# Queries and keys stored once per pair of heads, loaded in halves into even and odd partitions, with the transfer queue in program order from the first head's loads

## The chip, the cores and the metric

The kernel runs on one core of a Trainium2 chip. The time is that of one execution in device microseconds (us); shorter is better. A core has five engines with instruction streams of their own, which wait for each other by semaphores: TensorE (PE, matrix products; PEld is its loading of stationary operands), VectorE (DVE), ScalarE (ACT), GpSimd (POOL) and SyncE (SP), which here only issues transfers (DMAs). ACT issues transfers too; SPq and ACTq in the profile are these issues.

## The reference

One encoder block on a sequence of 1024 positions with 1024 channels, in float32:

```python
h = rmsnorm(x, g_mix) * (1 + scale1) + shift1          # scale, shift, gate from silu(c) @ w_ada
qa, ka, va, qb, kb, vb, ga, gb = split(h @ w_in)       # 8 + 8 heads of 64; two gates of 1024
oa = mixture_of_dilations(qa, ka, va, rel_bias)        # 8 heads: windows 128, 512, 2048 at strides 1, 4, 16
ob = neighbourhood_attention_2d(qb, kb, vb, na_rpb)    # 8 heads: 8 x 16 windows on a 16 x 64 grid
x = x + gate1 * ((sigmoid(ga) * (oa @ w_branch_dil) + sigmoid(gb) * (ob @ w_branch_na)) @ w_out)
h2 = rmsnorm(x, g_ffn) * (1 + scale2) + shift2
u = depthwise_conv3(h2 @ w_up)
x = x + gate2 * ((gelu(u_g) * u_v) @ w_down)
y = rmsnorm(x, g_final)
```

The outputs of an attention head are sums over exp(q·k/8 + bias) within its windows.

## The kernel before

**Numbers in two halves.** Float32 values go through PE as a high half (the value rounded to the matmul's format, made by ACT with a copy, L57 or L366) and a low half (the difference, made by DVE or POOL, L368, L61). A product is three matmuls: high by high, high by low, low by high; for the gates these are L84, L85 and L86.

**The stages, in order.** 0 to about 150 us: norm, conditioning, the values' projections and the first query/key projections (among them L308 and L310), with the order of all engines written out by hand. To about 297 us: the remaining query/key projections for pairs of heads, as products with seven instead of eight block multiplications (the generator `products`, L505 to L507; its sums and copies are L511 to L530); here a scheduler of the compiler orders each engine's instructions from its own estimates, and loads of weights (L723) go through SP. Then `fill(11)`, the first steps of the gate projections, and from 301 us the attention: 102 slots in a loop, each with transposes (T), scores (S) and outputs (O) of several heads in turn, with gate steps in between (`fill`). The rest (branch, output, up and down projections) runs to the end.

**Queries and keys.** A product gives two heads' queries (y = 0) or keys (y = 1) at once, head A on partitions 0 to 63 and head B on 64 to 127. `qk_evict` (pairs 0 to 3, the dilated heads) and `na_evict` (pairs 4 to 7, the neighbourhood heads) split them into halves (`split_qk`) and store them from ACT's queue into `q_scr`, `[16 heads, 3, 2, 64, 1024]`: for each head a tile of queries (high over low), one of the keys' high half twice, and one of their low half twice. So `qk_evict` issues two transfers for queries (L382) and four for keys (L379), one for each head and, for keys, each half; `na_evict` two times two (L406, L403). In all 80 stores: 64 of 256 KB and 16 of 512 KB.

`qk_load` brings a head back with three transfers of 512 KB on SP (L411) into the tiles `qs`, `ks` and `kl`: 128 partitions, the upper 64 the second copy. A score (dilated heads: L1028 and L1029) is then two matmuls over 128 partitions, (high; low) queries by (high; high) keys, and the same by (low; low) keys.

**Before the first score.** SP's and POOL's order is written by hand in one block: the first head's loads, `lnm`, the biases of head 0 (L701, L702), its values `vv` (L689 to L692; ACT copies them in two halves at L789, and splits follow), the biases of head 1. The next part of the program opens manual order for PE, ACT and DVE (`att`) and for SP (`att_sp`), ahead of `fill(11)`. Among the instructions of `fill(11)` are SP's load of weight tile 26 (L65) and the store of a gate tile `gs` (L1326, copied out by ACT at L1324); the load of tile 27 follows. These and the first head's block are separate hand-written pieces, and between pieces the scheduler may choose. In the compiled program tile 26, `gs` and tile 27 stand in SP's stream ahead of the first head's loads. A weight tile is split on ACT at L961 when its turn comes.

**Completion semaphores.** In the compiled program SP's and ACT's transfers share eight completion semaphores in turn, and a transfer first waits for the landing of the one eight before it in the scheduled order.

Of the kernel before, what the change touches and what calls it, by code (L numbers as in the profile page):

```python
# [10 lines left out]
FT = mybir.dt.float32  # L11
# [6 lines left out]
S = 1024  # L18
# [11 lines left out]
def hybrid_encoder(tc, xT, c, w_ada, small, w_in, p1_bias, p23_bias, na_bias, ln2_mult, ident, w_br, w_out,  # L30
                   w_up, w_down, out):
    nc = tc.nc
    act, dve, pool, pe, sp = nc.scalar, nc.vector, nc.gpsimd, nc.tensor, nc.sync
# [3 lines left out]
    dram = tc.alloc_tile_pool(name="scr", bufs=1, space=DRAM)  # L37

    def f(ap):
        return ap.bitcast(FT)  # L40
# [47 lines left out]
    halves = [slice(0, 512), slice(512, 1024)]  # L88
# [54 lines left out]
    def pair_load(j, i):  # L143
        wt = wada_tile(j)
        sp.dma_start(wt, w_ada[j][:, 2 * i:2 * i + 2])
        return [wt[:, t] for t in range(2)]
# [65 lines left out]
    def x_load(hf):  # L212
        x = []
        for k in range(0, KT, 2):
            if hf == 0:
                x2k = qkpool.tile([128, 2, 512], FT, name=("ks", "qb")[k // 6], bufs=(4, 2)[k // 6])
                raw_h[0].append(x2k)
                sp.dma_start(x2k, xT[hf, k // 2])
                x += [x2k[:, i] for i in range(2)]
            else:  # L220
                for i in range(2):
                    x.append(h_tile(FT))
                    sp.dma_start(x[-1], xT[hf, k // 2][:, i])
        return x
# [76 lines left out]
    def v_wide(*sts):  # L301
        ps = [ps_s.tile([128, 512], FT, name="pv", bufs=3) if len(sts) == 1 else ps_g.tile([128, 512], FT, name="pj")
              for _ in sts]
        for k in range(KT):
            whi, wlo = (t[:, :, k] for t in v_all)
            for st, p in zip(sts, ps):
                hhi, hlo = (t[:, st % 4 * 128:st % 4 * 128 + 128] for t in h[st // 4, k])
                pe.matmul(p, hhi, whi, start=k == 0, stop=False)  # L308
                pe.matmul(p, hhi, wlo, start=False, stop=False)
                pe.matmul(p, hlo, whi, start=False, stop=k == KT - 1)  # L310
        return ps
# [47 lines left out]
        banks = [ps_s.tile([128, 512], FT, name="pv", bufs=3) for _ in range(2)]  # L359
        return [banks[st // 2][:, st % 2 * 256:st % 2 * 256 + 256] for st in range(4)]  # L360

    q_scr = dram.tile([16, 3, 2, 64, S], FT, name="qks")

    def split_qk(y, dst, src):
        hi, lo = dst
        act.activation(hi, src, AF.Copy, scale=(1.0, 0.125)[y])  # L366
        if y:
            dve.scalar_tensor_tensor(lo, src, 0.125, f(hi), OP.mult, OP.subtract)  # L368
        else:
            dve.tensor_tensor(lo, src, f(hi), OP.subtract)  # L370

    def qk_evict(pr, y, hf, p, tag):
        st = qkpool.tile([128, 2, 512], FR, name=tag)
        split_qk(y, (st[:, 0], st[:, 1]), p)
        for i in range(2):
            a, dst = slice(64 * i, 64 * i + 64), q_scr[2 * pr + i][..., halves[hf]]
            if y:
                for x_ in range(2):
                    act.dma_start(dst[1 + x_].rearrange("b p s -> p b s"),  # L379
                                  f(st)[a, x_:x_ + 1].to_broadcast([64, 2, 512]))  # L380
            else:
                act.dma_start(dst[0].rearrange("b p s -> p b s"), f(st)[a])  # L382

    na_st = {}

    def na_evict(pr, y, hf, p):
        first = (pr, y) not in na_st
        if first:
            na_st[pr, y] = [qkpool.tile([128, S], FR, name="qs") for _ in range(2)]
        st = na_st[pr, y]  # L390
        if y:
            split_qk(y, [t.rearrange("p (w t r) -> p r w t", w=16, t=16)[:, 2 * hf:2 * hf + 2] for t in st],
                     p.rearrange("p (r w t) -> p r w t", r=2, w=16))
        else:
            for r in range(2):
                split_qk(y, [t.rearrange("p (c w r t) -> p r c w t", c=4, w=16, r=4)[:, 2 * hf + r] for t in st],
                         p.rearrange("p (r w c t) -> p r c w t", r=2, w=16, c=4)[:, r])
        if not first:
            for x_, t in enumerate(na_st.pop((pr, y))):
                for i in range(2):  # L400
                    src, dst = f(t)[64 * i:64 * i + 64], q_scr[2 * pr + i]
                    if y:
                        act.dma_start(dst[1 + x_].rearrange("b p s -> p b s"),  # L403
                                      src.rearrange("p (o s) -> p o s", o=1).to_broadcast([64, 2, S]))
                    else:
                        act.dma_start(dst[0, x_], src)  # L406

    def qk_load(head):
        qk = [qk2.tile([128, S], FR, name=n) for n in ("qs", "ks", "kl")]
        for y in range(3):  # L410
            sp.dma_start(f(qk[y]), q_scr[head, y].rearrange("b p s -> (b p) s"))  # L411
        return qk

    def q_blocks(qk):
        q = qk2.tile([128, S], FR, name="qb")
        for r in range(4):
            pool.tensor_scalar(q.rearrange("p (b r j) -> p r b j", b=8, r=4)[:, r],
                               f(qk[0][:, 256 * r:256 * r + 256]).rearrange("p (b j) -> p b j", b=8), 1.0, None,
                               OP.mult)
        qk.append(q)  # L420
# [113 lines left out]
    with tc.manual_schedule(engines={e.engine for e in (sp, act, dve, pool, pe)}):  # L534
        x = [x_load(0)]
# [103 lines left out]
        rows = {n: pair_load(*pairs[n]) for n in range(7)}  # L639
# [10 lines left out]
        for y in range(2):  # L650
            qk_evict(0, y, 0, qk_psum[y], "kl")
# [42 lines left out]
        def v_raw(load, head):  # L694
            vv = sm_pool.tile([128, 16, 128], FR, name="vv", bufs=2)
            load(head, f(vv[:, :, 64:128]))
            return vv

        def dil_bias(head):
            bt = sm_pool.tile([128, 896], FT, name="bias", bufs=4)  # L700
            sp.dma_start(bt[:, 0:512], p1_bias[head])  # L701
            sp.dma_start(bt[:, 512:896], p23_bias[head])  # L702
            return bt
# [33 lines left out]
        for n, step in enumerate(v_steps[:10]):  # L737
            if step is None:
                for ks in (slice(0, 4), slice(4, 8)):
                    for hv in range(2):  # L740
                        v_split(v_raws[hv], (dve, pool), ks, v_w[hv])
                raw[0] = p_load(0)
                ps = [ps_g.tile([128, 512], FT, name="pj") for _ in range(2)]
                for k in range(KT):
                    for p, w in zip(ps, qk_w):
                        product(p, w, lambda k: h[1, k], ks=[k])
                for y in range(2):
                    qk_evict(0, y, 1, ps[y], "kl")
                va_chunks(slice(0, 512))
                t_sums()  # L750
                prep = [a_operands(raw.pop(0), 4, p_home, p_sts[0], spot=p_spot)]
            else:
                p = v_wide(*step[1:])
            row_pairs(done_rows, row_ends[n])
            if step is not None:
                for st, pp in zip(step[1:], p):
                    v_out(step[0], st, pp, queue=act)
            done_rows = row_ends[n]
            if n in PREP:
                next(prep[0])  # L760
# [94 lines left out]
    qk2 = tc.alloc_tile_pool(name="qk2", bufs=2, reuse_waits="tile")  # L855
    at_pool = tc.alloc_tile_pool(name="at", bufs=2, reuse_waits="tile")
    sm_pool = tc.alloc_tile_pool(name="sm", bufs=2, reuse_waits="tile")
    with tc.manual_schedule(engines={sp.engine, pool.engine}):
        qks = {0: qk_load(0)}
        lnm = sm_pool.tile([128, 384], FT, name="lnm", bufs=1)  # L860
        sp.dma_start(lnm, ln2_mult)
        biases = {0: dil_bias(0)}
        values = {0: v_raw(va_load, 0)}
        biases[1] = dil_bias(1)
        pool.tensor_tensor(biases[0][:, 512:896], biases[0][:, 512:896], lnm, OP.add)
        q_blocks(qks[0])
# [38 lines left out]
    def settle():  # L905
# [6 lines left out]
        scored.clear()  # L912

    qks[1] = qk_load(1)
    side, second, count, credit = collections.deque(), collections.deque(), [0, 0], [0]

# [447 lines left out]
    def fill(n, asides=True):  # L1364
        for _ in range(n):
            next(steps, None)
            if asides:
                catch_up(550)
# [2 lines left out]
        for job, args in jobs:  # L1371
            job(*args)

    att = contextlib.ExitStack()
    att.enter_context(tc.manual_schedule(engines={e.engine for e in (pe, act, dve)}))
    att_sp = contextlib.ExitStack()
    att_sp.enter_context(tc.manual_schedule(engines={sp.engine}))
    fill(11)
    for s in range(LAST + 1):
        now[0] = s  # L1380
# [18 lines left out]
    o = [[opool.tile([128, 4, S], FR, name=f"o0{n}") for n in ("hi", "lo")]]  # L1399
# [76 lines left out]
    rows, sums = {}, {}  # L1476
# [33 lines left out]
    for i in range(2 * KT):  # L1510
        m, hf = divmod(i, 2)
# [16 lines left out]
        p = []  # L1528
# [441 lines left out]
    with tc.manual_schedule(engines={dve.engine}):  # L1970
        for hf, cs in ((0, slice(0, 512)), (1, slice(0, 256)), (1, slice(256, 512))):
            n = cs.stop - cs.start
            late = []
            for m in range(KT):
                if hf == 0 and m + 2 < KT:
                    end_w[m + 2] = end_weights(m + 2)
                p = ps.tile([128, 512], FT, name="pj", bufs=6)[:, :n]
# [25 lines left out]
        hf, cs, bc = before  # L2003
# [8 lines left out]
        dst = out[:, :, halves[hf]][:, :, cs]  # L2012
# [114 lines left out]
```

## Time and profile before

| | |
|---|---|
| runs before | 1497.62, 1498.62 (median), 1502.53 us |
| profiled execution | 1500.84 us |
| its span, first to last instruction | 1499.0 us |
| mean granted PE clock | 0.99 |
| busy: PE, DVE, POOL, ACT | 1453.7, 949.3, 859.0, 792.4 us |
| transfers | 249.52 MB, 166 GB/s in the mean |

The profile's rows come from one execution. "L505 PE MATMUL pj<-op,kl" is the instruction of line 505 on PE, with output and inputs by the program's names. A bracket such as [7.57 <-DMA ks<-qks] says how long the engine had stood idle just before, and what ended it. The granted clock is the share of full speed at which PE was allowed to run.

### The profile page before, as it was taken

Reading aid. Unit: us, or ns where it says so; the run is one execution under the profiler, and the core shown is the slowest. Engines: PE = TensorE matmul, PEld = TensorE weight load, DVE = VectorE, ACT = ScalarE, POOL = GpSimd, SP = SyncE. Lnnn points to the kernel's source line nnn. Section 1 sums busy time; section 2 is a strip of 40 time slices with the busy share of each in tenths; the row PEclk is TensorE's granted clock in tenths of the full one; section 3 lists DMA queues with packets and bytes.
Section 4 is the critical chain, followed back from the end, with each engine's and each line's share of the span. In section 5 each row is a group of like instructions: output and inputs, shape, how many; then the busy total and the mean of one; then the engine's idle time right before and its main releaser. Section 6 shows DMA issues by size and latency. Waiting matters only on the chain.

```text
span 1499.0 us, 21282 instructions
## 1 busy us (share of the span) xinstructions
PE 1453.7 (97%) x7308; PEld 1225.6 (82%) x7308; DVE 949.3 (63%) x1793; ACT 792.4 (53%) x1479; POOL 859.0 (57%) x706
## 2 busy tenths in 40 slices
PE   9999999979999989999999999999999999999998
PEld 8888777768888878888888878888888888887788
DVE  7687433335655666766625798666666667787865
ACT  6625533257777766763335555444444447575542
POOL 4155655443545466522258858766666676988712
PEclk9999999989999999999999999999999999999999
DMA  9589467774655789667734413222222234532213
GB/s 370 211 317 329 136 180 235 206 243 129 204 160 158 230 250 283 199 224 261 232 134 155 134 43 108 93 84 76 85 76 85 84 134 144 197 123 89 100 45 113
DMA packets 133588, 249.52 MB, mean 166 GB/s; under 512 B 47813, under 2 KB 60741, under 8 KB 133445
## 3 DMA queue, kind: packets, MB, share of 16 engines
q1 hardware_dynamic: 120408, 218.99, 44.1%
q10 hardware_dynamic: 13072, 29.17, 6.7%
q8 instruction: 58, 0.95, 0.3%
q14 instruction: 50, 0.40, 0.1%
HBM read 185.60 MB, written 68.29 MB: 169 GB/s over the span
## 4 chain that ended last, share of the span: by engine, by line
PE 66%; DMA 12%; DVE 10%; ACT 4%; issue 3%; POOL 3%; ACTq 2%; SPq 1%; DVEq 0%; POOLq 0%
PE pj L505 12%; PE pj L506 11%; PE pj L507 11%; PE pj L84 7%; PE pj L86 7%; PE pj L85 7%; DMA qks<-qs 3%; PE O L1299 1%; DMA oraw<-w_ada 1%; PE T L1044 1%; DMA gs<-gs 1%; PE O L1109 1%; PE O L1056 1%; DMA qks<-kl 1%; PE T L1092 1%
## 5 line engine op out<-in xcount | busy, mean ns | idle before, releaser
L61 POOL TENSOR_TENSOR wlo<-wraw,whi 128x512 fp32r<-128x512 f32 (+1 forms) x90 | 114.8, 1299 | 132.3 <-ACT whi L57 130.4
L505 PE MATMUL pj<-op,wsh 128*128 128x512 f32 x408 | 158.5, 390 | 1.9 <-ACT wsh L57 1.9
L506 PE MATMUL pj<-op,wsh 128*128 128x512 f32 x408 | 158.7, 389 | 0.5 <-DVE op L1546 0.5
L507 PE MATMUL pj<-op,wsl 128*128 128x512 f32 x408 | 157.4, 389 | 0.0
L61 POOL TENSOR_TENSOR wsl<-big,wsh 128x512 fp32r<-128x512 f32 (+1 forms) x86 | 111.9, 1326 | 44.7 <-ACT wsh L57 39.8
L84 PE MATMUL pj<-h,whi 128*128 128x512 f32 x272 | 116.4, 428 | 0.0
L86 PE MATMUL pj<-h,wlo 128*128 128x512 f32 x272 | 107.6, 396 | 0.0
L85 PE MATMUL pj<-h,whi 128*128 128x512 f32 x272 | 107.5, 395 | 0.0
L1756 DVE SCALAR_TENSOR_TENSOR big<-pj,sm,big 128x512 f32<-128x512 f32 (+2 forms) x183 | 94.8, 562 | 16.5 <-ACT big L1750 15.6
L887 DVE CUSTOM_DVE_ANT_0 P<-S,bias 128x256 f32<-128x256 f32 x128 | 49.2, 421 | 78.1 <-PE S L1029 39.8
L505 PEld LDWEIGHTS pj<-op,wsh 128*128 128x128 f32 x408 | 76.6, 188 | 18.6 <-ACT wsh L57 2.7
L505 PE MATMUL pj<-op,whi 128*128 128x512 f32 x232 | 90.7, 391 | 0.3 <-ACT wc L511 0.3
L506 PE MATMUL pj<-op,whi 128*128 128x512 f32 x232 | 90.4, 390 | 0.2 <-DVE op L1576 0.2
L507 PE MATMUL pj<-op,wlo 128*128 128x512 f32 x232 | 90.3, 389 | 0.0
L506 PEld LDWEIGHTS pj<-op,wsh 128*128 128x128 f32 x408 | 76.6, 188 | 16.7 <-DVE op L1546 0.9
L61 POOL TENSOR_TENSOR wsl<-wraw,wsh 128x384 fp32r<-128x384 f32 (+1 forms) x46 | 56.8, 1256 | 57.5 <-ACT wsh L57 53.2
L507 PEld LDWEIGHTS pj<-op,wsl 128*128 128x128 f32 x408 | 76.6, 188 | 16.0 <-POOL wsl L61 0.2
L888 ACT ACTIVATE P<-P,st 128x256 f32<-128x256 f32 x128 | 64.0, 502 | 38.1 <-DVE st L887 37.8
L901 DVE TENSOR_TENSOR tl<-T,th 128x512 fp32r<-128x512 f32 (+3 forms) x120 | 76.0, 648 | 5.2 <-ACT th L897 5.2
L57 ACT ACTIVATE whi<-wraw 128x1024 fp32r<-128x1024 f32 (+2 forms) x48 | 47.5, 993 | 55.0 <-PE pj L85 33.7
L1750 ACT ACTIVATE big<-pj,sm 128x512 f32<-128x512 f32 x61 | 47.0, 773 | 54.5 <-DVE pj L526 32.2
L526 DVE TENSOR_TENSOR pj<-pj,wc 128x512 f32<-128x512 f32 x40 | 27.8, 694 | 71.5 <-PE pj L507 71.5
(478 smaller groups left out, 4569.2 us busy)
## 6 DMA issues: line engine op xcount, KB each, us to landing
wada<-w_ada SPq DMA_DIRECT2D x31, 512.0 KB
qks<-qs ACTq DMA_DIRECT2D x52, 256.0 KB
wraw<-w_in SPq DMA_DIRECT2D x24, 512.0 KB
big<-w_up SPq DMA_DIRECT2D x22, 512.0 KB
wraw<-w_up SPq DMA_DIRECT2D x22, 512.0 KB
big<-as SPq DMA_DIRECT2D x22, 512.0 KB
as<-big SPq DMA_DIRECT2D x21, 512.0 KB
qks<-qs ACTq DMA_DIRECT2D x16, 512.0 KB
```

Source lines behind the costliest of these rows:

```text
L57: act.activation(hi, raw, AF.Copy)
L61: lo_eng.tensor_tensor(lo[:, i:i + step], raw[:, i:i + step], f(hi)[:, i:i + step], OP.subtract)
L84: pe.matmul(psum, whi[:, k0 + k], mhi, start=k == 0, stop=False)
L85: pe.matmul(psum, whi[:, k0 + k], mlo, start=False, stop=False)
L86: pe.matmul(psum, wlo[:, k0 + k], mhi, start=False, stop=k == n - 1)
L505: pe.matmul(psum, whi[:, k], bhi, start=j < 4 and k == 0, stop=False, skip_group_check=True)
L506: pe.matmul(psum, whi[:, k], blo, start=False, stop=False, skip_group_check=True)
L507: pe.matmul(psum, wlo[:, k], bhi, start=False, stop=k == n - 1, skip_group_check=True)
L887: dve.tensor_tensor_reduce(pp, d, bias, -1.0, BIG, OP.add, OP.min, mi)
L888: act.activation(pp, pp, AF.Exp, bias=mi, scale=-1.0, accum_out=li)
L901: dve.tensor_tensor(tt[1][:m, :n], pt[:m, :n], f(tt[0])[:m, :n], OP.subtract)
L1756: dve.scalar_tensor_tensor(y[:, dst], src, wt, y[:, dst], OP.mult, OP.add)
```

## The change

`q_scr` becomes `[8 pairs, 4, 128, 1024]`: queries' high and low halves, keys' high and low halves, each once, both heads of a pair in one tile of 128 rows. `qk_evict` stores with one transfer of 512 KB, `na_evict` with two of 512 KB: 32 stores in all. `qk_load` takes a head's 64 rows with six transfers of 256 KB: row p of one half goes to partition 2p, of the other to 2p + 1; for keys the same rows are read twice. Queries and keys are arranged alike, so the sum over partitions has the same terms. The hand-written order of SP and that of PE, ACT and DVE now begin before the first head's loads, and POOL's block stays where it was; so SP's stream follows the program from those loads on: head 0's six loads, `lnm`, biases, values, biases of head 1, head 1's six loads, then tile 26, `gs`, tile 27.

```diff
-    q_scr = dram.tile([16, 3, 2, 64, S], FT, name="qks")
+    q_scr = dram.tile([8, 4, 128, S], FT, name="qks")
...
     def qk_evict(pr, y, hf, p, tag):
         st = qkpool.tile([128, 2, 512], FR, name=tag)
         split_qk(y, (st[:, 0], st[:, 1]), p)
-        for i in range(2):
-            a, dst = slice(64 * i, 64 * i + 64), q_scr[2 * pr + i][..., halves[hf]]
-            if y:
-                for x_ in range(2):
-                    act.dma_start(dst[1 + x_].rearrange("b p s -> p b s"),
-                                  f(st)[a, x_:x_ + 1].to_broadcast([64, 2, 512]))
-            else:
-                act.dma_start(dst[0].rearrange("b p s -> p b s"), f(st)[a])
+        act.dma_start(q_scr[pr, 2 * y:2 * y + 2].rearrange("x p s -> p x s")[:, :, halves[hf]], f(st))
...
             for x_, t in enumerate(na_st.pop((pr, y))):
-                for i in range(2):
-                    src, dst = f(t)[64 * i:64 * i + 64], q_scr[2 * pr + i]
-                    if y:
-                        act.dma_start(dst[1 + x_].rearrange("b p s -> p b s"),
-                                      src.rearrange("p (o s) -> p o s", o=1).to_broadcast([64, 2, S]))
-                    else:
-                        act.dma_start(dst[0, x_], src)
+                act.dma_start(q_scr[pr, 2 * y + x_], f(t))

     def qk_load(head):
+        pr, i = divmod(head, 2)
+        a = slice(64 * i, 64 * i + 64)
         qk = [qk2.tile([128, S], FR, name=n) for n in ("qs", "ks", "kl")]
         for y in range(3):
-            sp.dma_start(f(qk[y]), q_scr[head, y].rearrange("b p s -> (b p) s"))
+            rows = f(qk[y]).rearrange("(p b) s -> b p s", b=2)
+            for b in range(2):
+                sp.dma_start(rows[b], q_scr[pr, 1 + y if y else b, a])
         return qk
...
-    with tc.manual_schedule(engines={sp.engine, pool.engine}):
+    att = contextlib.ExitStack()
+    att.enter_context(tc.manual_schedule(engines={e.engine for e in (pe, act, dve)}))
+    att_sp = contextlib.ExitStack()
+    att_sp.enter_context(tc.manual_schedule(engines={sp.engine}))
+    with tc.manual_schedule(engines={pool.engine}):
         qks = {0: qk_load(0)}
...
-    att = contextlib.ExitStack()
-    att.enter_context(tc.manual_schedule(engines={e.engine for e in (pe, act, dve)}))
-    att_sp = contextlib.ExitStack()
-    att_sp.enter_context(tc.manual_schedule(engines={sp.engine}))
     fill(11)
```

## The prediction

> **What bounds the kernel now.** I read the page's head first, for who is the bound; then the waits of PE, for what keeps it from working; then windows around each long wait, for the granted clock there.
>
> ```profile
> span 1499.0 us, 21282 instructions
> PE 1453.7 (97%) x7308; PEld 1225.6 (82%) x7308; DVE 949.3 (63%) x1793; ACT 792.4 (53%) x1479; POOL 859.0 (57%) x706
> ```
>
> PE is busy for 97% of the span; the next engine is DVE with 63%. The change takes no work from PE, so it can pay in two ways only: PE's 45 us of idle time, and time in which PE ran at a lower clock. The waits of PE (engine, line waited at, releaser: total us, times, longest):
>
> ```profile
> PE S L1028 <- DMA ks<-qks: 7.6, 1, 7.6
> PE pj L505 <- ACT kl L57: 4.6, 2, 2.8
> PE T L1286 <- POOL P L1277: 4.1, 2, 3.1
> PE pj L505 <- ACT wc L511: 2.9, 3, 2.3
> PE pj L308 <- ACT h L244: 1.7, 1, 1.7
> ```
>
> The longest is the first score matmul, which waits for the first head's key tile. The second and fourth belong to the query/key products, where ACT also issues the stores of queries and keys. Windows (us, busy time of PE, PEld, DVE, ACT, POOL with instruction counts, granted clock, DMA share, GB/s):
>
> ```profile
> 66.00:70.00 4.00, 3.37 (x9) 2.46 (x8) 3.78 (x6) 3.37 (x7) 0.00 (x0) 0.62 0.21 67
> 177.30:184.00 6.70, 5.75 (x25) 4.45 (x25) 2.62 (x3) 2.01 (x3) 2.56 (x2) 1.00 0.88 259
> 218.00:222.00 4.00, 3.89 (x9) 3.11 (x10) 2.28 (x3) 1.58 (x3) 3.78 (x3) 0.50 0.52 139
> 222.00:226.00 4.00, 4.00 (x15) 3.12 (x15) 0.81 (x2) 0.61 (x1) 0.00 (x0) 0.75 0.99 244
> 264.00:268.00 4.00, 3.81 (x10) 2.98 (x11) 1.38 (x2) 0.13 (x1) 2.52 (x3) 0.62 0.60 230
> 309.00:317.00 8.00, 7.27 (x23) 5.45 (x24) 1.55 (x8) 3.02 (x9) 4.81 (x6) 0.55 1.01 271
> 330.00:510.00 180.00, 178.79 (x1142) 158.95 (x1141) 104.64 (x354) 136.58 (x374) 86.66 (x78) 1.00 0.60 178
> 510.00:600.00 90.00, 82.40 (x519) 72.62 (x518) 60.47 (x191) 62.22 (x167) 53.94 (x48) 1.00 0.85 258
> ```
>
> After four of the waits the clock falls: 0.62 behind the one of 1.7 us, 0.50 and then 0.75 behind 2.8 us, 0.62 behind 2.3 us, 0.55 behind 7.6 us. I price a stretch with a lowered clock at length times (1 − clock): 1.5 us for 66–70, 2.0 + 1.0 = 3.0 for 218–226, 1.5 for 264–268, 3.6 for 309–317. So a wait near 2 us costs about twice its length.
>
> **The first head's loads (301 to 316).** Now SP loads weight tile 26 early, stores a finished gate tile (gs), loads tile 27, and only then takes up the first head.
>
> ```profile
> SPq L1326 <- DMA qks<-qs: 15.9, 1, 15.9
> ...
> 278.41 0.33 SPq L65 DMA_DIRECT2D wraw<-w_in  x1
> ...
> 300.63 0.81 SPq L65 DMA_DIRECT2D wraw<-w_in  x1
> 301.53 0.50 SPq L411 DMA_DIRECT2D qs<-qks  x1
> ...
> 308.49 3.72 SPq L692 DMA_DIRECT2D vv<-v  x2
> ```
>
> The first row is SP's own wait: the gs store (L1326) sat 15.9 us for the landing of a key store that has nothing to do with it. The compiled program gives DMAs eight completion semaphores in turn, and a DMA waits for the one eight before it; everything behind it on SP waits too. The query load is thus issued at 301.53 although the score matmul needs it about then.
>
> ```profile
> 309.06 0.55 PE L1028 MATMUL S<-ks,qs 128*128 128x256 f32 x1 [7.57 <-DMA ks<-qks]
> ...
> 315.79 1.04 PE L1044 MATMUL T<-idt,P 128*128 128x128 f32 x4
> ...
> 317.37 0.28 PE L1028 MATMUL S<-ks,qs 128*128 128x256 f32 x1
> 317.49 0.28 PE L1029 MATMUL S<-kl,qs 128*128 128x256 f32 x1
> ...
> 317.84 0.40 PE L84 MATMUL pj<-h,whi 128*128 128x512 f32 x1
> 318.07 0.39 PE L85 MATMUL pj<-h,whi 128*128 128x512 f32 x1
> 314.61 0.63 ACT L789 ACTIVATE vv<-vv 128x512 fp32r<-128x512 f32 x1 [0.71 <-DMA vv<-v]
> 285.21 0.70 DVE L518 TENSOR_TENSOR pj<-pj,ks 128x512 f32<-128x512 f32 x1 [2.03 <-PE pj L507]
> 296.01 0.69 DVE L368 SCALAR_TENSOR_TENSOR qs<-pj,qs 128x512 fp32r<-128x512 f32 x1 [1.34 <-ACT qs L366]
> ```
>
> The wait begins at 309.06 − 7.57 = 301.49 less the filler's last matmul, about 301.3. From there to the first transpose T (315.79) stand 9 filler matmuls and 8 score matmuls. At full clock a filler step is 318.07 − 317.84 = 0.23 and a score step 0.12, together 3.0 us: T could start at 304.3. It starts 11.5 us later; that is the whole prize of this edit.
>
> After it, the order on SP is six loads of head 0, lnm, two biases, four value loads, two biases, head 1's six loads, and only then tile 26, gs and tile 27. The buffer for the queries is free after 285.21 + 0.70 = 285.9, so loading can start there. The first-head loads wait for the key stores eight before, which end with the products: the last one can be issued when DVE has made its low half, 296.01 + 0.69 = 296.70. By the count of eight in turn, the keys' low half waits for the first two of the last four stores and is there in time for 301.3; the first bias waits for the last store. A DMA lands about 2.4 us after its issue ends (the values: 308.49 + 3.72 = 312.21, used by ACT at 314.61). The store then lands at 296.70 + 0.62 + 2.4 = 299.7; two bias and four value issues at some 0.6 (0.50 for the query load above, 0.62 for a store below; the 3.72 of the last row is mostly waiting) end at 299.7 + 3.6 = 303.3 and land at 305.7. I add 0.5 for the transfers ahead of them in the queue. ACT copies both halves of the values before it makes the exponentials, so T comes 315.79 − 314.61 = 1.18 us behind: **307.4**, still 3.1 us late. ACT at the values is what is late next. Such a wait again lowers the clock: 2.2, between the 1.5 and 3.0 above. Gain 8.4 − 2.2 = 6.2. Tile 26 is now issued near 307 and lands near 311, where ACT, which splits it just after the first exponentials (L961), would want it near 309; behind that stand copies that PE waits for. One us for it: **−5.2**. Ends: −11.5 (everything in time) and −2 (the values as late as if still one wait longer, and 2 to 4 us for tile 26). The tensor engines' part of the attention region is opened earlier too; between the old and the new place nothing is emitted for PE, ACT or DVE, so that costs nothing.
>
> **The stores (59 to 297).** 80 stores become 32: a query eviction 2 to 1, a key eviction 4 to 1, in the neighbourhood heads 4 to 2. ACT issues them ahead of its own work:
>
> ```profile
> 61.26 3.51 ACTq L379 DMA_DIRECT2D qks<-kl  x4
> 64.82 0.69 ACT L244 ACTIVATE h<-pcol,ada 128x512 fp32r<-128x512 f32 x1 [3.58 <-DMA qks<-kl]
> ...
> 214.03 2.87 ACTq L406 DMA_DIRECT2D qks<-qs  x4
> 217.00 1.06 ACT L57 ACTIVATE kl<-xr 128x1024 fp32r<-128x1024 f32 x1 [2.52 <-issue]
> ...
> 259.55 3.94 ACTq L379 DMA_DIRECT2D qks<-qs  x4
> 263.54 0.60 ACT L511 ACTIVATE wc<-pj 128x512 f32<-128x512 f32 x1 [4.02 <-DMA qks<-qs]
> L382 ACTq DMA_DIRECT2D qks<-qs x12: 582/620/787, 254.8 to 294.7; - x12
> ```
>
> One issue takes 0.62 (the median of the last row, which is min/median/max in ns). A single store must wait for DVE's low half (0.70 above), which costs ACT up to 0.7 more; it is in the sums.
> At 61.26, a fixed order: 3.51 becomes 0.6 + 0.7, so h comes 2.2 us earlier. The 1.7 us wait and its clock loss (1.5), and a 0.6 wait of the next h behind it, go: at most 3.8; I take **−3.0**, since the steps after it are also paced by ACT and DVE (3.37 and 3.78 of the 4 us).
> At 214.03: 2.87 becomes 1.43, the wait 2.84 becomes 1.4. At 177 a wait of this kind left the clock at 1.00, so I also count most of the 3.0: 4.4 at most, taken 3.3. At 259.55: 3.94 becomes 1.3, the wait 2.3 becomes below 0.5: 1.8 + 1.5 = 3.3 at most, taken 2.5. The window 177–184 has 6.70 − 5.75 = 0.95 idle: 1.0 taken with small ones elsewhere. Together **−6.8**, between 0 and −9: this stage is ordered by the scheduler, and with fewer instructions it may choose another order. Fewer bytes written (16 stores of 512 KB and 64 of 256 KB before, 32 of 512 KB after: 16.8 instead of 25.2 MB) are worth nothing by themselves, for PE waits for no transfer there.
>
> A rule against this half of the sum: the Trainium skill, "TensorE: Matmul & The Clock Gate", section "Why this matters for your kernels", warns of idle gaps over about 3 us, so by it the waits of 1.7 to 2.8 us would have left the clock alone and their removal would be worth their length only. The trace disagrees (0.62, 0.50 and 0.62 behind them), though a lowered clock could have another cause there. By the rule the sum is in the rivals below.
>
> **The loads (301 to 605).** 3 of 512 KB become 6 of 256 KB per head: 48 more issues on SP at 0.5 or so, 1.5 us a head. In 330–510 PE is busy 178.79 of 180 us and nothing waits on SP: hidden under PE's work, and without that cover it would be 1.5 us for each head there. In 510–600 PE idles 7.6 us, 4.1 of it waiting for POOL P in two places. The chain of work there (start, us, what):
>
> ```profile
> 544.26 0.62 SPq L1188
> 544.92 8.89 DMA fb<-fcs
> ...
> 555.18 1.01 POOL P L1277
> ...
> 556.24 0.65 PE T L1286 x4
> ```
>
> The load of fb, which PE's T waits for over POOL, is issued on SP behind a head's loads (L411). 3 issues more ahead of it: 3 × 0.43 = **+1.3**, between 0 and 4 (both waits, and as much again in transfers).
>
> Sum: −5.2 − 3.0 − 6.8 + 1.3 = −13.7. The profiled execution took 1500.84 us (span 1499.0 and 1.8 around it), 2.2 over the median of the three runs: 1500.84 − 13.7 = 1487.1, less 2.2 is **1485**.
>
> **Rivals.**
> *Everything arrives in time.* Values before 303, so no wait at T: 11.5 + 3.8 + 4.4 + 3.3 + 1.0 = 24, with 2 for waits of under 1 us that the sum leaves out and nothing for the loads' issues: 1500.84 − 26 − 2.2 = 1473. For it: the new queue needs only 15 issues from 286. Against: the first bias behind the last store.
> *The clock does not follow these waits.* Of the gains taken, 0.7 at 65, 1.9 at 214 and 0.7 at 259 are clock. Without these 3.3 the sum is −10.4: 1488. This is what the rule of the clock page named above would give. Against: three windows out of three (66–70, 218–226, 264–268).
> *The products are re-ordered and give their gain back*, and the neighbourhood stage pays more: −5.2 − 3.0 + 2.5 + 4 gives −1.7: 1497, no change. For it: an ordering by estimates is not monotone.
> *Slower: the half-height loads.* If 256 KB from 64 rows into every second partition ran slower than 512 KB to all 128. In 510–600 the transfers take 85% of the time at 258 GB/s, so 0.86 us per 256 KB (258/0.85 = 303 GB/s), and 13.5 us are spare. Seven heads load 42 such pieces there, 36 us. If each took twice as long, 36 − 13.5 = 22.5 us would come on top of −13.7 − 2.2: about 1507. It decides from (13.5 + 13.7 + 4.5)/42 = 0.75 us more per piece, 1.6 us. Against: stores from 64 rows filled much of 177–184, at 259 GB/s with a share of 0.88, the same rate per share. The Trainium skill, "SBUF — State Buffer", section "Door 1: The DMA port swizzle", says that 64 neighbouring partitions reach 8 of 16 ports; by its formula every second partition reaches all 16, so the change would be free of this. No run here shows that.
>
> **The numbers.** My forecast 0.50 (its own range 1478 to 1492), everything in time 0.20, no clock gain 0.10, no change 0.12, slower 0.08. The range 1472 to 1498 holds the first four but for their edges. A measurement of this kernel can tell 0.3%, 4.5 us, from no change: faster is below 1494.1 (0.80), the same up to 1503.1 (0.12), slower above (0.08).
>
> **What would show it.** The first L411 load near 286 to 290 instead of 301.53; PE's first score matmul at 301 to 302 without a wait for a DMA; a wait of 2 to 4 us at the first T, released by ACT P or the values; the clock back at 1.00 in the windows 66–70 and 218–226; a single L379-like issue per eviction; PE's time in 510–600 within 3 us. Wrong if the first loads are still held (by stores that land late), if the waits at L505 move elsewhere in the products, or if the loads pile up after 510.

## The result and the profile after

| | runs | median | ratio to before (95%) |
|---|---|---|---|
| before | 1497.62 to 1502.53 | 1498.51 us | |
| changed | 1482.18 to 1483.17 | **1482.98 us** | 0.989 (0.9872 to 0.9908) |

Faster by 1%, as forecast (1485). The profiled execution took 1483.17 us, 17.7 less than that of before, where the sum said 13.7. The page and PE's waits of the changed kernel (its lines are 5 to 10 lower than before):

```profile
span 1481.3 us, 21309 instructions
PE 1448.3 (98%) x7308; PEld 1224.1 (83%) x7308; DVE 952.1 (64%) x1793; ACT 792.3 (53%) x1479; POOL 858.5 (58%) x706
PE T L1281 <- POOL P L1272: 4.4, 1, 4.4
...
PE O L1051 <- ACT th L892: 2.5, 1, 2.5
PE T L1039 <- ACT P L883: 1.7, 2, 1.6
PE pj L498 <- POOL wlo L61: 1.7, 1, 1.7
...
PE pj L496 <- ACT whi L57: 1.3, 1, 1.3
```

Of the five waits shown before, four are gone: the first score's (7.6), those at L505 (ACT kl and wc) and at L308. The one for POOL P has grown, and four are new: the first transpose T waits for ACT's exponentials, the first output matmul O for ACT's copy th, and early in the products, at 145 and 151 us, PE now waits for the high and the low half (whi, wlo) of a weight tile. PE has 12.3 us less idle time (span less busy time: 45.3 before, 33.0 after) and is busy 5.4 us less for the same matmuls, which is the clock (0.990 in the mean of the old trace, 0.994 in this one). Windows, columns as before:

```profile
60.00:67.00 7.00, 7.00 (x47) 6.29 (x47) 6.10 (x9) 4.84 (x9) 0.00 (x0) 1.00 0.39 148
205.00:225.00 20.00, 20.00 (x90) 16.59 (x89) 8.73 (x14) 8.95 (x13) 13.88 (x12) 1.00 0.56 211
245.00:256.00 11.00, 11.00 (x50) 9.11 (x49) 5.27 (x7) 3.82 (x5) 8.68 (x7) 1.00 0.22 85
300.00:304.00 4.00, 4.00 (x18) 3.54 (x17) 1.40 (x6) 2.76 (x9) 1.28 (x1) 0.57 0.60 154
536.00:540.00 4.00, 3.00 (x11) 2.69 (x12) 0.02 (x1) 2.01 (x4) 4.00 (x4) 0.50 1.00 344
```

In the three windows where stores held PE up before, it now works all the time at 1.00. The low clock has moved to 300 and to 536, behind the new wait at O and the longer one for POOL P. SP, ACT and PE around the first head:

```profile
256.06 2.28 SPq L402 DMA_DIRECT2D qs<-qks  x2
262.52 1.66 SPq L402 DMA_DIRECT2D ks<-qks  x2
275.21 1.66 SPq L402 DMA_DIRECT2D kl<-qks  x2
...
291.74 0.33 SPq L65 DMA_DIRECT2D wraw<-w_in  x1
...
289.18 0.63 ACT L780 ACTIVATE vv<-vv 128x512 fp32r<-128x512 f32 x1 [0.96 <-DMA vv<-v]
...
297.52 0.63 ACT L956 ACTIVATE whi<-wraw 128x512 fp32r<-128x512 f32 x1 [5.75 <-DMA wraw<-w_in]
...
290.35 0.33 PE L1039 MATMUL T<-idt,P 128*128 128x128 f32 x1 [1.56 <-ACT P L883]
...
298.78 0.36 PE L1051 MATMUL O<-th,vv 128*128 128x256 f32 x1 [2.55 <-ACT th L892]
```

The first head's loads now start 45 us earlier. ACT copies the second half of the values at 289.18, and T follows 1.17 us later, as it did before (1.18). Then ACT stands for 5.75 us waiting for weight tile 26, which SP issued at 291.74, and the copy th, queued behind it, comes late for O.

How far ahead each kernel stands, taken at the same matmuls in both traces (start there less start before, median over seven neighbours, us; the columns are times in the trace of before). The runs below are in it too:

| | 72 | 160 | 223 | 267 | 316 (T) | 330 | 540 | 620 |
|---|---|---|---|---|---|---|---|---|
| changed | −4.7 | −1.2 | −10.8 | −15.3 | −25.4 | −20.5 | −20.6 | −18.0 |
| stores and loads alone | −4.5 | −1.2 | −10.8 | −15.3 | −25.8 | −25.8 | −25.6 | −25.8 |
| order alone | −1.6 | 0.1 | −3.4 | −1.6 | −5.0 | 0.7 | 1.1 | −0.6 |
| order, tile 26 first | −1.4 | 0.3 | −0.7 | −2.6 | −4.7 | −4.7 | −4.4 | −5.9 |
| changed, tile 26 early | −4.5 | 0.0 | −9.6 | −14.1 | −23.0 | −21.6 | −21.0 | −20.4 |
| all stores in pieces | −2.7 | 1.8 | −5.4 | −9.4 | −14.0 | −8.8 | −8.7 | −8.4 |
| only late stores in pieces | −4.6 | −1.1 | −8.1 | −12.6 | −23.1 | −23.1 | −22.8 | −21.0 |
| stores by SP | −4.5 | 0.4 | −2.5 | −2.5 | −5.4 | −5.4 | −5.5 | −5.1 |
| twelve loads | −4.7 | −0.9 | −10.5 | −15.0 | −21.1 | −18.7 | −15.1 | −4.1 |
| five loads | −4.4 | 0.4 | −9.2 | −13.8 | −25.0 | −25.0 | −25.0 | −26.9 |
| three loads | −4.3 | −2.4 | −11.8 | −16.3 | −18.8 | −18.8 | −18.8 | −20.4 |

Such a difference has scatter. The changed kernel and the one with tile 26 early have the same instructions up to 160 and stand at −1.2 and 0.0 there. The two kernels with only the order moved have the instructions of before, in the same order on every engine, up to 267; yet they stand at −1.6 and −1.4 at 72, at −3.4 and −0.7 at 223, and at −1.6 and −2.6 at 267. At 72 the reason can be read: the wait at L308 is 1.69 us before and 1.67 and 1.70 in these two, but the granted clock in 66 to 70 is 0.62 before and 1.00 in both of them. So up to 3 us of a difference to the trace of before can be chance, and some 2 of the 15.3 at 267 probably are.

### The profile page after: what moved, and what is told of

Its sections match the earlier page's. It is cut to its first block, busy times and chain, and to the rows that moved or that the text cites. A ratio compares the mean times of both kernels' runs of the same rounds, so it can differ in the third digit from the quotient of the medians.

```text
span 1481.3 us, 21309 instructions
## 1 busy us (share of the span) xinstructions
PE 1448.3 (98%) x7308; PEld 1224.1 (83%) x7308; DVE 952.1 (64%) x1793; ACT 792.3 (53%) x1479; POOL 858.5 (58%) x706
## 4 chain that ended last, share of the span: by engine, by line
PE 76%; DVE 7%; DMA 5%; POOL 4%; ACT 3%; issue 3%; SPq 1%; ACTq 0%; DVEq 0%; POOLq 0%
PE pj L496 14%; PE pj L497 14%; PE pj L498 14%; PE pj L84 8%; PE pj L85 7%; PE pj L86 7%; PE O L1294 1%; PE O L1104 1%; PE O L1051 1%; PE T L1039 1%; PE T L1281 1%; PE T L1087 1%; DVE op L1648 1%; PE S L1252 1%; POOL wlo L61 1%
## 5 line engine op out<-in xcount | busy, mean ns | idle before, releaser
L498 PEld LDWEIGHTS pj<-op,wsl 128*128 128x128 f32 x408 | 76.7, 188 | 15.9 <-POOL wsl L61 0.2
```

What stands on the lines that cost most here:

```text
L498: pe.matmul(psum, wlo[:, k], bhi, start=False, stop=k == n - 1, skip_group_check=True)
```

## The experiments

**Stores and loads alone.** The changed kernel with the manual orders opened where they were before:

```diff
-    att = contextlib.ExitStack()
-    ...
-    with tc.manual_schedule(engines={pool.engine}):
+    with tc.manual_schedule(engines={sp.engine, pool.engine}):
         qks = {0: qk_load(0)}
...
+    att = contextlib.ExitStack()
+    ...
     fill(11)
```

> The new storage, stores and half loads, with the manual orders opened where they were before. My theory: the stores give some 15 us up to the end of the products, as in the changed kernel (its matmul that stood at 267.2 before came 15.1 us earlier). In this program the scheduler put weight tile 26 ahead of the first head's loads but the gs store behind them; if the loads were held by gs and the store whose semaphore it waited for, the first score has no wait here either, and with tile 26 early ACT does not wait for it: 1477 to 1481 us. Rival, the moved manual order is what frees the loads: the first score waits some 7 us again, about 1490.

Measured: **1474.55 us**, ratio 0.9842 (0.9829 to 0.9854), faster than the whole change by 8.4 us, and than the 1477 to 1481 that I expected. No wait at the first score, none for tile 26. SP in this run:

```profile
258.02 0.33 SPq L65 DMA_DIRECT2D wraw<-w_in  x1
258.40 5.03 SPq L402 DMA_DIRECT2D qs<-qks  x2
...
290.28 1.10 SPq L402 DMA_DIRECT2D kl<-qks  x2
291.48 0.52 SPq L1317 DMA_DIRECT2D gs<-gs  x1
```

Tile 26 goes first, the head's loads right behind it, gs after head 1's loads. Left to itself, the scheduler had dropped the bad order of before as soon as loads and stores were changed. Compared instruction by instruction, the compiled programs of this kernel and of the changed one differ in one place only: the load of tile 26 stands ahead of the first head's loads here, and 21 transfers later, behind head 1's, in the changed kernel. That one place is what sets the two apart: 5.3 us by 330 in the table (behind ACT's wait of 5.75: 2.55 + 0.28 of PE's, and the low clock of 300 to 304). The 2.5 more by 620 come with a longer wait for POOL P (4.41 against 2.60 us); the traces do not show how that hangs on tile 26.

**The order alone.** The kernel before with the manual orders opened ahead of the first head's loads:

```diff
+    att = contextlib.ExitStack()
+    ...
-    with tc.manual_schedule(engines={sp.engine, pool.engine}):
+    with tc.manual_schedule(engines={pool.engine}):
         qks = {0: qk_load(0)}
...
-    att = contextlib.ExitStack()
-    ...
     fill(11)
```

> The storage, stores and loads of before, with only the manual orders opened ahead of the first head's loads. My theory: the products keep their waits (1.7, 2.8, 2.3 us) and their low clock, the first score no longer waits, ACT waits for tile 26 after the first exponentials as in the changed kernel (it lost 4.9 us there from T to 324): net 4 to 6 us, 1492 to 1495. With three loads per head the wait at the neighbourhood heads' first T is that of before (3 us), not 4.4. Rival, the order is what pays: 1485 to 1488.

Measured: 1501.05 us, ratio 1.0012 (0.9998 to 1.0027): nothing gained. My expectation was wrong. PE's rows:

```profile
300.47 0.35 PE L1032 MATMUL S<-ks,qs 128*128 128x256 f32 x1 [1.02 <-DMA ks<-qks]
...
304.83 0.58 PE L1033 MATMUL S<-kl,qs 128*128 128x256 f32 x1 [4.00 <-DMA kl<-qks]
...
320.01 0.35 PE L1060 MATMUL O<-th,vv 128*128 128x256 f32 x1 [3.35 <-ACT th L901]
```

SP takes the first head's loads up at once, but in this compiled program each of them waits for the landing of one of the last key and query stores, of which there are still two or four to an eviction. The wait of 7.6 becomes 1.0 + 4.0, a lead of 5.0 is reached at T, and the wait for tile 26 takes it back (0.7 behind at 330).

**The order with tile 26 first.** As before this, with one more edit:

```diff
+        ahead[26] = w_load(w_in[26])
         qks = {0: qk_load(0)}
...
-                raw[n + 2] = w_load(w_in[26 + n])
+                raw[n + 2] = w_load(w_in[26 + n]) if n else ahead.pop(26)
```

> The manual orders moved as in the change, on the storage of before, with tile 26 loaded ahead of the first head's loads. Theory, tile 26 behind head 1's loads is what takes back the order's gain: the wait of 3.4 us at the first output matmul and the low clock behind it go, 1501 - 5 to 7: 1494 to 1496. Rival, the landing of the key stores is all that holds the first head: no change against the order alone, 1499 to 1502.

Measured: 1495.72 us, ratio 0.9986 (0.9972 to 1.0). As expected. The lead of 4.7 us at T stays to 620: on the old storage too, the place of tile 26 is worth some 5 us in the traces (0.7 behind against 4.7 ahead at 330). By the two ratios it is 4 us, at the edge of their intervals.

**Tile 26 early in the changed kernel.** The same edit, with the load behind `qk_load(0)`.

> The changed kernel with weight tile 26 loaded right behind the first head's keys, ahead of lnm, biases, values and head 1's loads. My theory: ACT's wait of 5.75 us for tile 26 goes, with it PE's wait of 2.55 us at the first output matmul and the low clock behind it (0.57 in 300 to 304, 1.7 us): 1483 - 4.5 = 1478.5, 1477 to 1480. Rival, another operand is as late: the wait stays at 1 to 2.5 us with another releaser, 1481 to 1483.

Measured: 1479.16 us, ratio 0.987 (0.9857 to 0.9883). That is within what I expected, but the interval overlaps that of the change (0.9872 to 0.9908), so what follows rests on the traces. The wait at O goes, but tile 26 now stands ahead of lnm, biases and values, and T waits 2.77 us for ACT's P instead of 1.56. Part of the prize moved to the values; in front of the first head's loads, where the kernel with stores and loads alone has it, it costs them nothing.

**All stores in pieces.** The changed kernel with 80 stores again, each byte written once:

```diff
-        act.dma_start(q_scr[pr, 2 * y:2 * y + 2]...[:, :, halves[hf]], f(st))
+        for i in range(2):
+            a = slice(64 * i, 64 * i + 64)
+            for xs in ((slice(0, 1), slice(1, 2)) if y else (slice(0, 2),)):
+                act.dma_start(q_scr[pr, 2 * y:2 * y + 2]...[a, xs, halves[hf]], f(st)[a, xs])
...
-                act.dma_start(q_scr[pr, 2 * y + x_], f(t))
+                for i in range(2):
+                    act.dma_start(q_scr[pr, 2 * y + x_, 64 * i:64 * i + 64], f(t)[64 * i:64 * i + 64])
```

> The changed kernel with every store cut into as many transfers as before (80 in all), each byte still written once. Theory, the number of issues on ACT: the waits behind ACT at 61 us and in the products come back and 8 to 13 of the 15 us with them: 1491 to 1496. Rival, the bytes written: no wait comes back, 1483 within 2. Rival, the scheduler's other order of the products: then the waits come with a different order and not behind runs of store issues on ACT, any time between.

Measured: 1492.84 us, ratio 0.9957 (0.9943 to 0.997); 5.9 us of the lead at 267 are gone (15.3 to 9.4), fewer than the 8 to 13 expected. The total fell within the range for other reasons as well: the key loads again wait for the stores in pieces (1.5 and 2.9 us at the first scores), so the gain of the first head is smaller too. What an issue costs ACT, from the groups of the tile qks (min/median/max in ns), first of the changed kernel, then of this one:

```profile
L393 ACTq DMA_DIRECT2D qks<-qs x16: 326/327/353, 171.7 to 226.4; - x16
L375 ACTq DMA_DIRECT2D qks<-qs x12: 366/367/403, 233.5 to 279.7; - x12
```

```profile
L378 ACTq DMA_DIRECT2D qks<-qs x36: 452/608/1149, 240.2 to 287.9; - x36
L397 ACTq DMA_DIRECT2D qks<-qs x32: 452/609/1557, 174.7 to 236.9; - x32
```

A store of 512 KB from all 128 partitions is issued in 0.33 to 0.37 us, one of 128 or 256 KB from 64 partitions in 0.61 (median). With three loads (below), where two stores of 512 KB often follow each other, the medians by line are 0.36 to 0.49. Which property of a store sets this time, the runs do not separate.

**Only the neighbourhood heads' stores in pieces**, on the manual orders of before (the second half of the last diff alone):

> The new storage with the manual orders of before (1474.6), but the stores of the neighbourhood heads' queries and keys (177 to 240 us) cut in two as before, those of the dilated heads whole. PE's order in the products is that of the kernel with all stores in pieces. Theory, ACT's issues act where they stand: at 67 us the gain of the change (3.5 to 4.5) is whole, the gain between 177 and 222 us falls to 2 to 4 of the 6, the gain around 264 is whole: the matmul that stood at 267.2 comes 11 to 13 us early instead of 15; 1477 to 1479. Rival, the other order of the products is what gains: the same 9.6 as with all stores in pieces.

Measured: 1479.43 us, ratio 0.9876 (0.986 to 0.9892). PE's order of instructions is exactly that of the kernel with all stores in pieces, so the two differ in the products only by what ACT issues: 3.2 us of lead at 267. The early part (−4.6 at 72) is as in the change. It lies where the stores lie, as the theory of ACT's issue time had it, and the rival (no difference) does not fit. At 72 this is plain: −4.6 against −2.7, where the five kernels with whole stores and the change's order of the products lie between −4.4 and −4.7. At 267 those five spread over 1.5 us (−13.8 to −15.3), so the 3.2 are more than scatter, but not by far.

**The stores issued by SP**, on the kernel before, in `qk_evict` (both calls) and likewise in `na_evict`:

```diff
-                act.dma_start(dst[0].rearrange("b p s -> p b s"), f(st)[a])
+                sp.dma_start(dst[0].rearrange("b p s -> p b s"), f(st)[a])
```

> The kernel before with its 80 stores issued by SP instead of ACT: same number, same bytes, only ACT relieved. My theory, ACT's time in issuing (72 us before, 15 after, between 50 and 302 us) is what the products pay: the matmul that stood at 267.2 comes 10 us or more earlier, close to the 15 of the changed kernel, as far as SP's own loads are not delayed. Rival, number or bytes of the transfers: no more than 3 us earlier there. The whole time depends also on SP's first loads of the attention, 1484 to 1494.

Measured: 1495.39 us, ratio 0.9975 (0.9961 to 0.999). Only 2.5 us at 267, as the rival had it, and no more than the kernels with only the order moved show there by chance. But this does not tell the theories apart:

```profile
197.58 5.68 SPq L403 DMA_DIRECT2D qks<-qs  x4
203.37 2.00 SPq L723 DMA_DIRECT2D wraw<-w_in  x1
...
216.38 0.79 PE L505 MATMUL pj<-op,kl 128*128 128x512 f32 x1 [2.37 <-ACT kl L57]
```

Four stores hold SP for 5.68 us while a weight tile waits behind them, and PE waits in the products as before. The stalled queue was moved from one engine to another.

**Three loads.** New stores from 128 partitions, but keys written twice into rows that lie next to each other, queries likewise side by side, so that a head comes back with three loads of 512 KB:

```diff
-    q_scr = dram.tile([8, 4, 128, S], FT, name="qks")
+    q_scr = dram.tile([8, 2, 128, 2, S], FT, name="qks")
+    q_rows = dram.tile([8, 128, 2, S], FT, name="qks2")
...
+        sp.dma_start(f(qk[0]), q_rows[pr, a].rearrange("p b s -> (p b) s"))
+        for y in (1, 2):
+            sp.dma_start(f(qk[y]), q_scr[pr, y - 1, a].rearrange("p b s -> (p b) s"))
```

> New stores from all 128 partitions, but keys stored twice with rows next to each other (48 stores, 25.2 MB as before) so that a head comes back with three loads of 512 KB as before; manual orders of before. Theory, the number of issues counts on both queues: 16 more stores cost ACT 6 us of issue and PE at most 3 us in the products, 48 loads less bring the neighbourhood stage to PE's waits of before or less: 1472 to 1477. Rival, the bytes of the stores: the products lose 5 us or more, 1479 and up.

Measured: 1480.62 us, ratio 0.9887 (0.9869 to 0.9906). As many bytes are written as before (25.2 MB), and the products are as far ahead as in the change (−16.3 at 267): **the bytes cost nothing that shows**. What it loses comes later, and puts the total where the rival had it for another reason:

```profile
SPq L1320 <- ACT gs L1318: 19.1, 1, 19.1
...
282.69 0.33 SPq L1320 DMA_DIRECT2D gs<-gs  x1
283.12 0.37 SPq L65 DMA_DIRECT2D wraw<-w_in  x1
283.59 0.40 SPq L403 DMA_DIRECT2D qs<-qks  x1
...
290.26 0.55 PE L1022 MATMUL S<-ks,qs 128*128 128x256 f32 x1 [5.51 <-DMA ks<-qks]
```

Here the scheduler put gs and tile 27 ahead of the first head's loads again, and the wait of before is back at 5.5 us, without the old stores. So gs ahead of the loads is enough for it: SP stood 19.1 us until ACT had copied out gs, and the loads stood behind it.

**Five loads**, keys as in the change and only the queries side by side:

```diff
-    q_scr = dram.tile([8, 4, 128, S], FT, name="qks")
+    q_scr = dram.tile([8, 2, 128, S], FT, name="qks")
+    q_rows = dram.tile([8, 128, 2, S], FT, name="qks2")
...
+        sp.dma_start(f(qk[0]), q_rows[pr, a].rearrange("p b s -> (p b) s"))
+        for y in (1, 2):
```

> The new storage and stores with the manual orders of before (1474.6) and a head's queries in one load of 512 KB from rows stored next to each other: five loads a head. Theory, one load less frees 0.5 us of SP for each head: the first transpose's wait (1.2 us) goes and the wait at POOL P near 530 falls by 0.5 to 1.5: 1472 to 1474. Rival, the sixth load is hidden: 1474 to 1476.

Measured: 1473.03 us, ratio 0.9834 (0.9818 to 0.9849). The first transpose's wait is gone, that for POOL P is 2.0 us. Against 0.9842 for six loads the intervals overlap: not shown to be faster.

**Twelve loads** of 128 KB a head, on stores and loads alone:

```diff
             for b in range(2):
-                sp.dma_start(rows[b], q_scr[pr, 1 + y if y else b, a])
+                for c in range(0, S, 512):
+                    sp.dma_start(rows[b][:, c:c + 512], q_scr[pr, 1 + y if y else b, a, c:c + 512])
```

> The new storage and stores with the manual orders of before (1474.6), each head loaded with twelve transfers of 128 KB instead of six of 256 KB. Theory, each extra load costs SP 0.4 to 0.6 us, hidden until 510, and delays the fb loads once: the wait of 2.6 us at POOL P grows by 2.5 to 3.5 us and may lower the clock: 1477 to 1481. Rival, the bytes alone count: 1473 to 1476.

Measured: 1492.9 us, ratio 0.9968 (0.9952 to 0.9984): 18 us lost, not 3 to 6. The waits:

```profile
PE T L1278 <- DVE tl L893: 8.0, 4, 3.7
PE T L1036 <- ACT P L880: 4.1, 1, 4.1
```

The first transpose waits 4.1 us because the values stand behind more loads; between 540 and 620 alone the lead falls by 11 us. A head's loads now take SP some 7.4 us to issue (2.39 + 2.51 + 2.45 for head 1), against 3.4 for six. Their rows are also half as long, but the transfers were not the limit: in 510 to 600 they moved 232 GB/s at a share of 0.79, against 258 at 0.87 with six, the same rate per share. So the number of loads is hidden only up to some point, which lies between 6 and 12.

**The fb loads earlier.** With five loads, the last dilated pair's fb loads two slots earlier, ahead of the next neighbourhood head's loads, and then (25) one slot:

```diff
-                at(s0 + 26, "first", self.load, 1, z)
+                at(s0 + (24 if pr == 3 else 26), "first", self.load, 1, z)
```

> The new storage and stores with the manual orders of before (1474.6); a head's queries in one load of 512 KB from rows stored next to each other, so five loads a head, and the fb loads of the last dilated pair issued behind their own stores, ahead of the next neighbourhood head's loads. Theory: the wait of 2.6 us at POOL P and the low clock behind it (1.7 us) go: 1470 to 1472. Rival, the head's loads, now 3 us later, are waited for instead: 1474 or more.

> As the kernel with five loads, and the fb loads of the last dilated pair one slot earlier (ahead of a weight tile's load, behind the next neighbourhood head's). Theory: the wait at POOL P falls below 1.5 us and no low clock follows: 1471 to 1473. Rival, another wait takes its place, as with fb two slots earlier: 1474 to 1476.

Measured: 1475.38 us, 0.9842 (0.9821 to 0.9864), and 1473.38 us, 0.9838 (0.9821 to 0.9855). With two slots the wait for POOL P goes, and two waits for DVE tl of 2.3 and 1.6 us take its place: DVE had stood 4.66 us for a bias of the next neighbourhood head, which is loaded behind fb here, so in substance the rival. With one slot the wait for POOL P stays, at 3.4, with no other in its place, so neither theory nor rival fits. No gain is shown in either (1473.03 without the edit).

## Why the prediction was right, and where it was not

**Right in the sum, in part by luck.** 1485 against 1482.98. PE's idle time and its clock were the two sources, and the clock is 1.00 in the three windows named. The first score has no wait, T a short one, fb a longer one. The profiled execution moved 17.7 us, 4.0 more than my 13.7; half of that did not show in the medians, since the old profile was 2.2 over its median and the new one is 0.2 over. By the table, 15.3 us came up to 267 (forecast 9.8) and 5.2 more up to 330 (forecast 5.2), and 2.5 were lost again by 620 (forecast 1.3). The stores' term was short, in part only against an unlucky old trace, and the first head's came out because two errors of 3.9 us in it cancelled (below).

**The stores: right cause, size too small.** I took 3.0 + 6.8 = 9.8 and bounded it by 13; the table has 15.3 at 267, and 12.7 to 13.7 against the two kernels with the old order of the products. Nor did it come where I put it. The store at 61 us gave what I took, some 3 us at 72 against those two kernels (−4.7 against −1.6 and −1.4), but only 1.2 us of lead are left at 160: PE caught up with the first product's weight tile and waited 1.3 us for whi and 1.7 for wlo, which it did not before. So in part the waits moved elsewhere in the products, one of my signs of being wrong. Between 160 and 267 stand 14.1 us where I had 6.8. The mis-sized step is the issue: 0.62 us taken for one store (that was the row of a 64-partition store, the nearest), 0.33 to 0.37 measured. ACT issued transfers for 72.3 us between 50 and 302 us before, for 14.6 after (sum over all its issues in the trace). At 61 the store took 0.38 and h came 3.2 us earlier, where I had 2.2; the waits of 2.84 and 2.34 went (0.3 us is left of the one for wc), not down to 1.4 and 0.5. What gives the 15 is not split to the end: pieces against whole stores for the dilated heads, in the same order of PE, are 3.2 us for 23 us of ACT's issues (54.1 against 31.1). Between the kernel before and all stores in pieces lie 9.4 us at 267 with 18 us less issue time, another order of the products and fewer bytes; bytes are excluded by the kernel with three loads, the other two are not separated.

**The first head: right in the net, wrong in the cause.** I took SP's wait of 15.9 us, for the landing of a store, as what held the loads. It was not the last wait of gs:

```profile
SPq L1326 <- ACT gs L1324: 5.5, 1, 5.5
...
296.00 3.52 ACTq L379 DMA_DIRECT2D qks<-qs  x4
299.57 0.60 ACT L1324 ACTIVATE gs<-pj 128x512 f32<-128x512 f32 x1 [3.60 <-DMA qks<-qs]
```

After the landing, gs waited 5.5 us more for its own copy, which stood in ACT's queue behind four issues of key stores. So what held the loads at the end were ACT's issues and the place of gs; the change shortens the first, and gs no longer stands ahead of the loads in it.

I gave the moved order 5.2 us (8.4 at T, less 2.2 of clock and 1 for tile 26). From 267 to T the lead grew by 10.1 (I had 6.2), and 4.9 were lost by 330 (I had 1): net 5.2. But the step "that is the whole prize of this edit" failed. With the new stores and loads the whole prize, 10.5 us, was there without the edit, since the scheduler no longer put gs and tile 27 ahead; and with the old stores the edit gave nothing. What the edit did in the changed kernel was to move tile 26 behind head 1's loads, **which costs 8.4 us** in the medians, 5.3 of them by 330. I saw that term and priced it at 1 us, by tile 26 landing 2 us later than ACT would want it. Counted from the first score, I had it issued at +5.7, landing at +9.7 and wanted at +7.7. It was issued at +6.2, but landed near +11.8, since six loads of head 1 stood ahead of it in the queue, and ACT was through with the exponentials at +6.2: a wait of 5.75 us. The copies behind it, which PE waits for, were named; the landing was what I mis-sized. I had not asked whether the scheduler's order would survive the first two edits; without the third the kernel took 1474.55.

**The loads: right for 6, wrong beyond.** I took +1.3 in the neighbourhood stage. The wait for POOL P grew by 1.34 (3.07 to 4.41). The change lost 2.6 between 540 and 620 with the low clock behind it; six loads without the moved order lost nothing, five gained 1.9, three 1.6. So 0 to 3, as bounded. The slower rival, half-height loads at half the rate, did not come about (258 GB/s at a share of 0.87 in 510 to 600 with stores and loads alone, at 0.85 before).

**The clock.** In all four stretches in which I expected it back it is back, and it fell in two new ones. Of the 17.7 us, 5.4 are PE's own busy time. But the step "a wait near 2 us costs about twice its length" was drawn from one execution and does not hold. In the two kernels with the old order of the products, the wait of 1.7 us at L308 left the clock at 1.00 both times, the one of 2.8 at L505 lowered it in one of them, and PE was busy 1451.3 and 1448.9 us, 2.4 and 4.8 less than in the trace of before, without the new stores. So part of the 5.4 is that trace's bad luck. The mean clock was 0.992 over 17 runs of before and 0.994 over the four of the change: by this estimate some 3 of PE's 1450 us. The rival without a clock gain had the right doubt for the wait at L308; its time, 1488, was not met.

## What to carry to other kernels

Look at how long an engine stands issuing a transfer, not only at the transfer's bytes: one store from all 128 partitions took ACT 0.35 us here, four from 64 partitions took 2.4 to 3.9, and PE paid for it. A kernel's lead at one place needs more than one trace: the same instructions stood up to 3 us apart here, since the clock did not fall behind the same waits each time. When an edit changes the number of transfers, an automatic order around it can change with it, so take the edits one by one on the chip before crediting a gain to any of them. Where a queue is put in program order, go through every load that falls back in it: one weight tile 21 places later cost a third of what the rest had won.

## What was not expected of the hardware

The same wait does not always lower the clock. In the kernel before and in the two with only the order moved, the same matmul at L505 waits nearly the same time: 2.84, 2.84 and 2.83 us. That of before has 0.50 in 218 to 222; the windows of the order alone and of the order with tile 26 first:

```profile
216.00:220.00 4.00, 2.84 (x12) 2.29 (x13) 1.36 (x2) 2.55 (x3) 2.82 (x3) 1.00 0.51 173
```

```profile
216.00:220.00 4.00, 2.63 (x6) 2.15 (x7) 1.14 (x2) 2.56 (x3) 2.60 (x3) 0.52 0.50 175
```

One keeps the full clock, the other falls to half. Over all 14 traces, by the granted clock of the 6 us after PE's waits (beyond 55 us): it fell behind 14 of 14 waits above 3.3 us, 13 of 15 between 2.3 and 3.3, and 6 of 50 between 1.4 and 2.3. In 18 of the 27 long ones that it followed, the mean of these 6 us was 0.72 to 0.78, so some 1.7 us lost, and 0.50 to 0.55 in the other nine, some 3 us. So a wait between 1.4 and 2.3 us seldom cost clock here, and one above 2.3 nearly always. The Trainium skill says in "TensorE: Matmul & The Clock Gate", section "What's actually happening", that the clock is decided over windows of about 3.4 us that run free of the program. The traces fit this, since then it matters where in a window a wait falls, but no run here shows the windows themselves. They disagree with that page's section "Why this matters for your kernels", which warns of idle gaps over about 3 us: here the change lies near 2.3.
